# The down projection of a conditioned decoder layer as seven block products

## The chip, the cores and the metric

The kernel runs on one core of one Trainium2 chip, as one launch. The metric is device time in microseconds (us) of that core. All arithmetic is float32 at the interfaces; the engines are TensorE (PE, its weight loads PEld), VectorE (DVE), ScalarE (ACT), GpSimd (POOL) and SyncE (SP), which here only issues DMAs.

## The reference

The program is one inference step of a decoder layer with a DeltaNet branch, a sliding-window attention branch and a gated feed-forward part, for 1024 prompt tokens and 8 sample tokens (1032 columns in the kernel). Only the feed-forward part and the final norm bear on the change:

```python
h2 = _rmsnorm(x, lp['norm2_w']) * (1 + sc2) + sh2
gate = h2 @ lp['w_ffn_gate']                      # 1024 -> 2816
up = h2 @ lp['w_ffn_up']                          # 1024 -> 2816
gate_ext = jnp.concatenate([ffn_prev, gate], axis=1)
gc = _causal_dwconv(gate_ext, lp['ffn_conv_w'], L) + lp['ffn_conv_b']
x = x + gt2 * ((jax.nn.silu(gc) * up) @ lp['w_ffn_down'])   # 2816 -> 1024
...
y_prompt = _rmsnorm(xp, final_norm_w)
y_sample = _rmsnorm(xs, final_norm_w)
```

## The kernel before

**A product in float32.** Every operand of a large product is split in two parts: ScalarE copies it, rounded, as the high part (line 127), and VectorE subtracts that from the operand, which gives the low part (line 128). `mm3` then issues three matmuls for a tile: high by high (line 178), weight high by data low (179), weight low by data high (180). Data stand with features on the partitions and tokens along the columns. The 1032 columns are taken in four quarters of 256, 256, 260 and 260 (`QUARTERS`), the last eight of the last quarter being the sample tokens. A quarter of one row block of 128 outputs fills one bank of PSUM.

**Gate and up.** The 2816 features are 22 tiles of 128, taken as 11 pairs. For a pair, `pair_weights` loads two raw tiles of the weights and lets GpSimd make four of the weight sums (line 1525, buffers `ws`, three of them), which are split; `pair_product` then computes two feature tiles by two row halves by Strassen's seven products instead of eight, once for the first two quarters and once for the last two. Its operands stand split in rooms of 128 x 2080 elements, which fourteen tags name (`bmh0` to `bmh3`, `bml0` to `bml2`, `pk0` to `pk6`). ScalarE copies products that go to more than one place (line 1562), VectorE adds and multiplies at the end (lines 1605 to 1639). The result of the silu times up, `fa`, goes from SBUF to a DRAM tensor `act`, a half at a time, issued by SP.

**Down.** `ffn_down` takes the 22 feature tiles in groups of 4, 4, 4, 4, 2 and 4. For each tile it loads 128 rows of the weight (4 KB each) and the tile of `act`, both issued by SP, and splits both into rooms that the gate and up projections no longer need. Then, for each of 8 row blocks and 4 quarters, one bank collects the group's matmuls (twelve, or six for the group of two), in seven banks in turn, and VectorE adds the bank, times the gate, to the residual `x1` of that row block and quarter (`add_gated`, line 1406; for the sample columns lines 1410 and 1411, which go by a small tile `gtmp`). That is 192 such adds. Two of the row blocks of `x1` stay in SBUF from before; six are loaded from DRAM at the start of this stage, by ScalarE's queue. In the last group the quarters come in the order third, fourth, first, second, and after a quarter's last row block `norm_rows` does the final norm of its tokens: transposes on TensorE (line 188), sums of squares on ScalarE (line 1741), a scaling on VectorE and ScalarE (lines 1764 and 1761), and the output DMAs.

**The order.** A scheduler places the operations of the whole program on each engine's queue by due times, not by the order in the source, and can thus start the down projection's matmuls between the last ones of the up projection, or put a split ahead of an add. Each engine then runs its queue in that order; an instruction that waits holds up what stands behind it on the same engine.

## Time and profile before

| | us |
|---|---|
| three runs | 2182.31, 2189.14, 2196.92 |
| median | 2189.14 |
| the profiled execution | 2191.09 |
| its span | 2189.4 |

The windows of the profile cut the span by stage: up to 1485 us the two branches (the first row has the last part of them), from there to 1925 gate and up, to 2180 down and the final norm. Around the last two, whose own rows stand with the prediction:

```profile
1000.00:1485.00 485.00, 474.32 (x3435) 459.87 (x3434) 237.00 (x523) 146.52 (x330) 51.16 (x59) 0.96 0.45 132
2180.00:2189.40 9.40, 1.04 (x6) 0.42 (x4) 2.39 (x6) 3.07 (x10) 0.70 (x1) 0.81 0.30 112
```

A row gives the window, its length, busy us (and instructions) of PE, PEld, DVE, ACT and POOL, the clock that the throttle granted to TensorE as a share of full speed, the mean share of time in which the 16 DMA engines were busy, and the GB/s moved. In rows of instructions, "x2" behind a form is a count, the bracket is the engine's idle time ahead of it and what ended that, and buffer numbers are left out of the names.

### The profile page before, as it was taken

How to read it: one execution, taken by the hardware profiler on the slowest of the kernel's cores; microseconds unless marked ns; L12 is line 12 of the kernel's file. 1: busy time of each engine (PE TensorE's matmuls, PEld its weight loads, DVE VectorE, ACT ScalarE, POOL GpSimd, SP SyncE). 2: the span in 40 equal slices, each digit the busy share in tenths (PEclk: the TensorE clock that was granted, in tenths of full speed). 3: DMA queues.
4: the chain of work that ended last, by engine and by line, in shares of the span. 5: the costliest groups of instructions: out<-in, count | busy, mean ns of one | idle time of the engine just before them, and what ended most of it. 6: DMA issues, size and time to landing. Idle time of an engine off the chain costs nothing. (4 is left out here: it accounts for less than half of the span.)

```text
span 2189.4 us, 41264 instructions
## 1 busy us (share of the span) xinstructions
PE 2114.4 (97%) x16573; PEld 1996.0 (91%) x16573; DVE 1332.6 (61%) x2892; ACT 800.5 (37%) x2037; POOL 298.5 (14%) x395
## 2 busy tenths in 40 slices
PE   7999999999999999999999999999999999999998
PEld 4985887899898998898999999999999999999998
DVE  4656666374465655675324565478876876866565
ACT  3655446234234243333322032244433433421102
POOL 1000000021221111111110300002333232100000
PEclk8999999999999989999999999899999999999999
DMA  7256442141332222222226854413232222363202
GB/s 275 80 139 219 131 138 84 60 123 43 80 82 63 63 55 57 47 67 54 82 95 196 244 162 138 140 59 98 78 91 74 78 90 67 99 223 123 88 3 79
DMA packets 271346, 228.16 MB, mean 104 GB/s; under 512 B 57566, under 2 KB 237697, under 8 KB 271138
## 3 DMA queue, kind: packets, MB, share of 16 engines
q1 hardware_dynamic: 269826, 221.23, 33.4%
q10 hardware_dynamic: 1152, 3.70, 0.4%
q8 instruction: 130, 2.13, 0.4%
q14 instruction: 62, 0.51, 0.1%
q0 software_dynamic: 176, 0.59, 0.1%
HBM read 175.51 MB, written 52.35 MB: 104 GB/s over the span
## 5 line engine op out<-in xcount | busy, mean ns | idle before, releaser
L178 PE MATMUL mm<-b1h,wh 128*128 128x384 f32 (+1 forms) x1392 | 456.9, 329 | 4.6 <-ACT z L764 2.2
L180 PE MATMUL mm<-b1h,wl 128*128 128x384 f32 (+1 forms) x1392 | 452.2, 325 | 3.8 <-DVE wl L128 3.8
L179 PE MATMUL mm<-b1l,wh 128*128 128x384 f32 (+1 forms) x1392 | 449.8, 323 | 0.0
L178 PEld LDWEIGHTS mm<-b1h,wh 128*128 128x128 f32 x1392 | 263.1, 189 | 14.0 <-issue 4.7
L180 PEld LDWEIGHTS mm<-b1h,wl 128*128 128x128 f32 x1392 | 263.1, 189 | 10.3 <-issue 5.5
L179 PEld LDWEIGHTS mm<-b1l,wh 128*128 128x128 f32 x1392 | 263.5, 189 | 3.1 <-issue 2.8
L127 ACT ACTIVATE wh<-raw 128x1024 fp32r<-128x1024 f32 x75 | 78.6, 1048 | 157.9 <-PE mm L179 79.6
L128 DVE TENSOR_TENSOR wl<-raw,wh 128x1024 fp32r<-128x1024 f32 x74 | 90.4, 1221 | 66.0 <-ACT wh L127 65.3
L178 PE MATMUL mm<-pk,w 128*128 128x260 f32 (+1 forms) x440 | 124.4, 283 | 0.7 <-ACT pk L127 0.6
L179 PE MATMUL mm<-pk,w 128*128 128x260 f32 (+1 forms) x440 | 124.2, 282 | 0.8 <-DVE pk L128 0.8
L178 PE MATMUL mm<-b2h,wh 128*128 128x384 f32 (+1 forms) x384 | 123.3, 322 | 1.1 <-ACT wh L127 1.1
L180 PE MATMUL mm<-pk,w 128*128 128x260 f32 (+1 forms) x440 | 124.2, 282 | 0.0
L180 PE MATMUL mm<-b2h,wl 128*128 128x384 f32 (+1 forms) x384 | 121.9, 320 | 1.1 <-DVE wl L128 1.1
L179 PE MATMUL mm<-b2l,wh 128*128 128x384 f32 (+1 forms) x384 | 122.7, 320 | 0.0
L1406 DVE SCALAR_TENSOR_TENSOR x<-mm,mT,x 128x256 f32<-128x256 f32 (+2 forms) x133 | 63.4, 481 | 76.7 <-PE mm L180 74.5
L180 PE MATMUL mm<-bmh,pk 128*128 128x256 f32 (+1 forms) x380 | 109.8, 289 | 0.0
L178 PE MATMUL mm<-bmh,pk 128*128 128x260 f32 (+1 forms) x380 | 109.7, 289 | 0.0
L179 PE MATMUL mm<-bml,pk 128*128 128x260 f32 (+1 forms) x353 | 102.1, 289 | 0.0
L178 PE MATMUL mm<-bmh,w 128*128 128x260 f32 (+1 forms) x320 | 91.9, 287 | 0.0
L180 PE MATMUL mm<-bmh,w 128*128 128x260 f32 (+1 forms) x320 | 91.7, 287 | 0.0
L128 DVE TENSOR_TENSOR w<-ws,w 128x512 fp32r<-128x512 f32 x88 | 60.1, 684 | 41.6 <-ACT w L127 41.6
L178 PEld LDWEIGHTS mm<-pk,w 128*128 128x128 f32 x440 | 82.6, 188 | 1.4 <-ACT pk L127 0.8
(600 smaller groups left out, 5807.1 us busy)
## 6 DMA issues: line engine op xcount, KB each, us to landing
raw<-in_w_in_dram SPq DMA_DIRECT2D x60, 512.0 KB
bml<-act SPq DMA_DIRECT2D x22, 516.0 KB
raw<-in_w_ffn_gate_dram SPq DMA_DIRECT2D x22, 512.0 KB
raw<-in_w_ffn_up_dram SPq DMA_DIRECT2D x22, 512.0 KB
raw<-in_w_ffn_down_dram SPq DMA_DIRECT2D x22, 512.0 KB
qst<-in_w_mod_dram SPq DMA_DIRECT2D x16, 512.0 KB
raw<-in_w_mod_dram SPq DMA_DIRECT2D x16, 512.0 KB
raw<-in_x_prompt_dram SPq DMA_DIRECT2D x12, 512.0 KB
```

Source lines behind the costliest of these rows:

```text
L127: self.nc.scalar.activation(hi, x, AF.Copy)
L128: (eng or self.nc.vector).tensor_tensor(lo, x, hi.bitcast(F32), op=ALU.subtract)
L178: mm(ps, whi, xhi, start=first, stop=False, **kw)
L179: mm(ps, whi, xlo, start=False, stop=False, **kw)
L180: self.last_mm = mm(ps, wlo, xhi, start=False, stop=last, **kw).ins
L1406: nc.vector.scalar_tensor_tensor(x[:, :np_], ps[:, :np_], self.mT[:, m + j, 8:9], x[:, :np_], op0=ALU.mult, op1=ALU.add)
```

## The change

**What is computed.** The 22 feature tiles are again taken as 11 pairs, and the product of the weight (two feature tiles of a pair by two halves of 512 outputs) with the activations (two feature tiles by two halves of the columns) by Strassen's seven block products. One product of one pair is a step: four row blocks `j` times two column pieces `p`, so eight banks, three matmuls in each. A product keeps its eight banks, all that PSUM has, over all 11 pairs. Products 4 and 7 share their banks without a restart: after 4 the banks, which then hold product 4, are added to one quarter of the output, and after 7, holding the sum of both, to another; so it is with 3 and 5. The products are run in the order 4, 7, 3, 5, 1, 2, 6, which makes 77 steps. What stands in the banks after products 4, 7 and 6 goes to one quarter of the output, after 3, 5, 1 and 2 to two (`home`). For these ScalarE copies a bank to SBUF and VectorE adds the copy twice; for the former VectorE adds from the bank. `less` is the gate with its sign turned, for homes that subtract.

**Operands.** Five products need a sum or difference of two weight blocks; GpSimd makes it, in place, in the raw slot, from two blocks loaded by SP. Five of the seven activation operands are sums or differences too: GpSimd makes them during gate and up, as soon as a half of a pair is done (`act_operands`), into a tile `sums`, and issues a DMA of them to a new DRAM tensor `xd`, which takes the place of `act`; the other two go there by SP. Each step loads its operand, 128 x 516, and its weight block, 128 x 512, into one raw slot, which is split into one of 13 rooms. There are three raw slots and two halves of the tile `bmh0`. Before, a tile of `w` or `act` was loaded once; now a tile pair is read once for each product.

**The rest.** The six row blocks of `x1` are loaded by GpSimd's queue, behind the fetch of step 5, instead of ScalarE's. The last product runs bank after bank, 33 matmuls in each, in three banks in turn, the second piece of columns first, with the final norm woven in between. `copies`, a tile of the gate and up projections, is now also what ScalarE copies the banks to.

```diff
-    def add_gated(self, t, ps, j, m):
-
-        nc = self.nc
+    def add_gated(self, t, ps, j, m, by=None):
+
+        nc = self.nc
+        by = self.mT[:, m:m + 8, :] if by is None else by
         lo, n = QUARTERS[t]
         np_ = min(n, NP - lo)
         x = self.x1_cols(j, lo, n)
-        nc.vector.scalar_tensor_tensor(x[:, :np_], ps[:, :np_], self.mT[:, m + j, 8:9], x[:, :np_],
+        nc.vector.scalar_tensor_tensor(x[:, :np_], ps[:, :np_], by[:, j, 8:9], x[:, :np_],
                                        op0=ALU.mult, op1=ALU.add)
...
             done[p, i] += 1
-            if done[p, i] == 4:
-                c, n = HALF[p]
-                nc.sync.dma_start(self.act[f + i][:, c:c + n], a[i][:, c:c + n])
+            if done[p, 0] == done[p, 1] == 4:
+                self.act_operands(p, f // 2, a)
 
         self.pair_product(psum, w, (0, 1), up)
+
+    def act_operands(self, p, g, a):
+
+        nc = self.nc
+        c, n = HALF[p][0], QUARTERS[2 * p][1]
+        (a1, b1), (a2, b2) = ((x[:, c:c + n], x[:, c + n:c + 2 * n]) for x in a)
+        sums = self.sums[:, 5 * p:5 * p + 5, :n]
+        for i, x, y, op in ((0, a1, b2, ALU.add), (1, b1, b2, ALU.add), (2, a1, a2, ALU.add),
+                            (3, b1, a1, ALU.subtract), (4, a2, b2, ALU.subtract)):
+            nc.gpsimd.tensor_tensor(sums[:, i], x, y, op=op)
+        for i, x in ((5, a1), (6, b2)):
+            nc.sync.dma_start(self.xd[i, g][:, c // 2:c // 2 + n], x)
+        nc.gpsimd.dma_start(self.xd[0:5, g, :, c // 2:c // 2 + n].rearrange("i p n -> p i n"), sums)
...
-        for f0, f1 in ((0, 4), (4, 8), (8, 12), (12, 16), (16, 18), (18, FT)):
-            fs = range(f0, f1)
-            ws, acts = [], []
-            for f in fs:
-                raw = self.t(self.pw, [P, NP], "raw", bufs=3)
-                nc.sync.dma_start(raw, I["w_ffn_down"][0][f * P:(f + 1) * P, :])
-                ws.append(room(0, f, NP))
-                self.split(*ws[-1], raw)
...
-                if f == 0:
-                    for j in range(2, 8):
-                        nc.scalar.dma_start(self.x1[j], self.x1d[j])
...
-            order = [(j, t) for t in (2, 3, 0, 1) for j in range(8)] if last else \
-                [(j, t) for j in range(8) for t in range(4)]
-            for j, t in order:
...
-                for i, ((wh, wl), (ah, al)) in enumerate(zip(ws, acts)):
-                    self.mm3(ps, wh[:, j * P:(j + 1) * P], wl[:, j * P:(j + 1) * P], ah[:, c:c + n], al[:, c:c + n],
-                             i == 0, i == len(acts) - 1)
-                self.add_gated(t, ps, j, 40)
...
+        G, n = FT // 2, NT // 2
+        tags = ("bmh2", "bml0", "bml2", "bmh1", "pk2", "bml1", "pk3", "pk6", "pk4", "pk0", "pk5", "pk1", "bmh3")
+        made = {5: (2, (1, 1)), 3: (5, (0, 1), (1, 1), ALU.subtract), 4: (6, (1, 0), (0, 0), ALU.subtract),
+                7: (4, (1, 0), (1, 1), ALU.add), 1: (0, (0, 0), (1, 1), ALU.add), 2: (1, (0, 0)),
+                6: (3, (0, 0), (0, 1), ALU.add)}
+        chains = ((4, 7), (3, 5), (1,), (2,), (6,))
+        home = {3: ((0, 0, 1), (1, 1, 1)), 5: ((1, 0, 1), (0, 0, -1)), 4: ((0, 1, 1),), 7: ((0, 0, 1),),
+                1: ((0, 0, 1), (1, 1, 1)), 2: ((0, 1, 1), (1, 1, -1)), 6: ((1, 1, 1),)}
+        steps = [(i, g) for c in chains for i in c for g in range(G)]
+        ready = {}
+        less = []
+
+        def fetch(s):
+            i, g = steps[s]
+            if s % 5 == 3:
+                ready["raw"] = self.t(self.bm, [P, KC, QW], "bmh0").rearrange("p k n -> p (k n)")
+            raw = self.t(self.pw, [P, n + 512], "raw", bufs=3) if s % 5 < 3 else \
+                ready["raw"][:, (s % 5 - 3) * 1040:(s % 5 - 3) * 1040 + n + 512]
+            at, *src = made[i]
+            src = [x if type(x) is not tuple else
+                   I["w_ffn_down"][0][(2 * g + x[0]) * P:(2 * g + x[0] + 1) * P, 512 * x[1]:512 * x[1] + 512] for x in src]
+            nc.sync.dma_start(raw[:, n:], src[0])
+            if len(src) > 1:
+                other = self.t(self.pw, [P, 512], "ws", bufs=3)
+                nc.sync.dma_start(other, src[1])
+                nc.gpsimd.tensor_tensor(raw[:, n:], raw[:, n:], other, op=src[2])
+            nc.sync.dma_start(raw[:, :n], self.xd[at, g])
+            room = self.room(tags[s % len(tags)], [P, KC * QW])
+            hi, lo = room[:, :n + 512], room[:, n + 512:2 * (n + 512)]
+            self.split(hi, lo, raw)
+            ready[s] = hi, lo
+            if s == 5:
+                less.append(self.t(pool, [P, KC, 9], "less"))
+                nc.gpsimd.tensor_scalar(less[0], self.mT[:, 40:48, :], -1.0, None, op0=ALU.mult)
+                for j in (2, 3, 4):
+                    self.x1[j] = self.t(pool, [P, NT], f"x1_{j}")
+                for j in range(2, 8):
+                    nc.gpsimd.dma_start(self.x1[j], self.x1d[j])
+
+        def step(s, ps, p, j, first, last, kw):
+            hi, lo = ready[s]
+            x, w = slice(256 * p, 256 * p + 256 + 4 * p), slice(n + j * P, n + j * P + P)
+            self.mm3(ps, hi[:, w], lo[:, w], hi[:, x], lo[:, x], first, last, **kw)
+
+        def take(ps, i, p, j):
+            if len(home[i]) > 1:
+                self.turn = (self.turn + 1) % KC
+                r = self.copies[:, self.turn, :256 + 4 * p]
+                nc.scalar.copy(r, ps)
+                ps = r
+            for d, q, sign in home[i]:
+                self.add_gated(2 * p + q, ps, j + 4 * d, 40, self.mT[:, 40:48, :] if sign > 0 else less[0])
+
+        banks = [(self.pmm, "mm", 2), (psum, "wv", 2), (psum, "wy", 2)] * 2 + [(self.pmf, "mm", 1), (psum, "nr", 1)]
+        order = [(p, j) for j in range(4) for p in range(2)]
+        s = done = 0
+        for c in chains[:-1]:
+            ps = {(p, j): self.t(pl, [P, 512], tag, bufs=k)[:, :256 + 4 * p] for (p, j), (pl, tag, k) in zip(order, banks)}
+            for i in c:
+                for g in range(G):
+                    while done < min(s + len(tags), len(steps)):
+                        fetch(done)
+                        done += 1
+                    for p, j in order:
+                        step(s, ps[p, j], p, j, g == 0 and i == c[0], g == G - 1, {"skip_group_check": True} if i != c[0] else {})
+                        if g == G - 1:
+                            take(ps[p, j], i, p, j)
+                    s += 1
+        while done < len(steps):
+            fetch(done)
+            done += 1
+        self.ffn_rows(pool, psum)
+        tail = self.norm_rows(pool, psum, [2 * P, 3 * P])
+        chunks = [[0], [P], [], [], [4 * P, 5 * P], [6 * P, 7 * P, NP], [], []]
+        for k, (p, j) in enumerate((p, j) for p in (1, 0) for j in range(4)):
+            ps = self.t(self.pmf if k % 3 == 2 else self.pmm, [P, 512], "mm", bufs=1 if k % 3 == 2 else 2)[:, :256 + 4 * p]
+            for g in range(G):
+                step(s + g, ps, p, j, g == 0, g == G - 1, {})
+            take(ps, 6, p, j)
+            for c in chunks[k]:
+                for _ in self.norm_rows(pool, psum, [c]):
+                    pass
+            for _ in range({5: 6, 6: 1}.get(k, 0)):
+                next(tail)
+        for _ in tail:
+            pass
...
-            self.act = self.t(self.dr, [FT, P, NT], "act")
+            self.xd = self.t(self.dr, [7, FT // 2, P, NT // 2], "xd")
...
+                        self.sums = self.t(pool2, [P, 10, QW], "r")
...
-                                self.copies = self.t(pool2, [P, KC, QW], "r")
...
-            x1 = {j: self.t(pool, [P, NT], f"x1_{j}") for j in (5, 6, 7, 2, 3, 4)}
-            self.x1 = xj + [x1[j] for j in range(2, 8)]
+            x1 = {j: self.t(pool, [P, NT], f"x1_{j}") for j in (5, 6, 7)}
+            self.x1 = xj + [x1.get(j) for j in range(2, 8)]
```

Where the change moves instructions, in the order of each engine's queue. First GpSimd, one steady pair of the gate and up projections, before; `raw` are the two loaded weight tiles, `ws` the sums:

```order
L1525 TENSOR_TENSOR ws_18951<-raw_18931,ws_18941 128x512
L1525 TENSOR_TENSOR ws_19190<-raw_19180,raw_19182 128x512
L1525 TENSOR_TENSOR ws_19192<-ws_19190,raw_19180 128x512
L1525 TENSOR_TENSOR ws_19200<-raw_19180 128x512
L1525 TENSOR_TENSOR ws_19202<-raw_19182,ws_19192 128x512
L1525 TENSOR_TENSOR ws_19421<-raw_19411,raw_19413 128x512
```

and after, with `fa` the two feature tiles of the pair, `r` the tile `sums`, and `xd` the DRAM tensor:

```order
L1526 TENSOR_TENSOR ws_20758<-ws_20756,raw_20746 128x512
L1655 TENSOR_TENSOR r_15585<-fa_20038,fa_20039 128x256
L1655 TENSOR_TENSOR r_15585<-fa_20039 128x256
L1655 TENSOR_TENSOR r_15585<-fa_20038,fa_20039 128x260
L1655 TENSOR_TENSOR r_15585<-fa_20039 128x260
L1655 TENSOR_TENSOR r_15585<-fa_20038,fa_20039 128x256
L1655 TENSOR_TENSOR r_15585<-fa_20038 128x256
L1655 TENSOR_TENSOR r_15585<-fa_20038,fa_20039 128x260
L1655 TENSOR_TENSOR r_15585<-fa_20038 128x260
L1526 TENSOR_TENSOR ws_20766<-raw_20746 128x512
L1658 DMA xd_14275<-r_15585 128x5x256
L1658 DMA xd_14275<-r_15585 128x5x260
```

Between the second and the third weight sum of a pair there now stand eight operand sums (the other two are ahead of this piece), and the two DMAs stand behind the third. Next VectorE, where the down projection's first adds stand; `x_0` and `x_1` are row blocks of the residual, `pk` and `bml` rooms of split operands. Before:

```order
L128 TENSOR_TENSOR pk_2846_21386<-raw_21384,pk_2846_21386 128x1024
L1406 SCALAR_TENSOR_TENSOR x_0_2332_15579<-mm_20912,mT,x_0_2332_15579 128x256
L1406 SCALAR_TENSOR_TENSOR x_0_2332_15579<-wv_20926,mT,x_0_2332_15579 128x256
L128 TENSOR_TENSOR pk_2850_21396<-raw_21394,pk_2850_21396 128x1024
L1406 SCALAR_TENSOR_TENSOR x_0_2332_15579<-wy_20940,mT,x_0_2332_15579 128x260
L1406 SCALAR_TENSOR_TENSOR x_0_2332_15579<-mm_20954,mT,x_0_2332_15579 128x252
L1410 TENSOR_TENSOR gtmp_20968<-mm_20954,mT 128x8
L1406 SCALAR_TENSOR_TENSOR x_1_2333_15580<-mm_20971,mT,x_1_2333_15580 128x256
L128 TENSOR_TENSOR pk_2853_21405<-raw_21403,pk_2853_21405 128x1024
L1406 SCALAR_TENSOR_TENSOR x_1_2333_15580<-wv_20985,mT,x_1_2333_15580 128x256
L1406 SCALAR_TENSOR_TENSOR x_1_2333_15580<-wy_20999,mT,x_1_2333_15580 128x260
```

After, at the end of product 4:

```order
L128 TENSOR_TENSOR bml_2844_21226<-raw_21220,bml_2844_21226 128x1028
L128 TENSOR_TENSOR bmh_2847_21259<-raw_21253,bmh_2847_21259 128x1028
L128 TENSOR_TENSOR pk_2850_21292<-raw_21286,pk_2850_21292 128x1028
L1407 SCALAR_TENSOR_TENSOR x_0_2332_15579<-mm_20997,mT,x_0_2332_15579 128x256
L1407 SCALAR_TENSOR_TENSOR x_0_2332_15579<-wv_20998,mT,x_0_2332_15579 128x252
L1411 TENSOR_TENSOR gtmp_21467<-wv_20998,mT 128x8
L1407 SCALAR_TENSOR_TENSOR x_1_2333_15580<-wy_20999,mT,x_1_2333_15580 128x256
L1407 SCALAR_TENSOR_TENSOR x_1_2333_15580<-mm_21000,mT,x_1_2333_15580 128x252
L1412 TENSOR_TENSOR x_0_2332_15579<-x_0_2332_15579,gtmp_21467 128x8
L1411 TENSOR_TENSOR gtmp_21478<-mm_21000,mT 128x8
L1412 TENSOR_TENSOR x_1_2333_15580<-x_1_2333_15580,gtmp_21478 128x8
L128 TENSOR_TENSOR bml_2853_21325<-bmh_2851_21319,bml_2853_21325 128x1028
```

The adds, which came in at every bank of twelve matmuls between splits, now come eight in a row at the end of a product, behind the splits of steps up to the 18th. Last TensorE, in the down projection. Before, six of the twelve matmuls that one bank takes in a row over the four feature tiles of a group:

```order
L180 MATMUL wy_21148<-bmh_2794_20875,pk_2792_20870 128x256
L178 MATMUL wy_21148<-bml_2797_20890,pk_2796_20886 128x256
L179 MATMUL wy_21148<-bml_2797_20890,pk_2796_20886 128x256
L180 MATMUL wy_21148<-bml_2797_20890,pk_2796_20886 128x256
L178 MATMUL wy_21148<-bmh_2801_20900,pk_2799_20895 128x256
L179 MATMUL wy_21148<-bmh_2801_20900,pk_2799_20895 128x256
```

After, at the start of product 7, with rooms that hold steps 11 to 13:

```order
L178 MATMUL mm_20997<-bmh_2836_21128 128x256
L179 MATMUL mm_20997<-bmh_2836_21128 128x256
L180 MATMUL mm_20997<-bmh_2836_21128 128x256
L178 MATMUL mm_20997<-bmh_2839_21161 128x256
L179 MATMUL mm_20997<-bmh_2839_21161 128x256
L178 MATMUL wv_20998<-pk_2833_21119 128x260
```

Where a bank took its whole group of tiles, it now takes the three matmuls of one step or, as here, of two and part of a third, before the next bank gets its turn.

34 lines of the change are left out of this document (1 added, 33 removed).

## The prediction

> **What bounds the kernel now.** First the page's busy times and the chain of waits, then the stage that is changed by windows, then single instructions there. The page gives
>
> ```profile
> span 2189.4 us, 41264 instructions
> PE 2114.4 (97%) x16573; PEld 1996.0 (91%) x16573; DVE 1332.6 (61%) x2892; ACT 800.5 (37%) x2037; POOL 298.5 (14%) x395
> ```
>
> and the windows of the gate and up projections (first row) and of the down projection with the final norm (second row):
>
> ```profile
> 1485.00:1925.00 440.00, 436.49 (x3645) 435.17 (x3644) 339.37 (x582) 183.59 (x359) 124.15 (x122) 1.00 0.29 90
> 1925.00:2180.00 255.00, 255.00 (x2149) 254.33 (x2147) 149.36 (x356) 42.50 (x64) 3.86 (x7) 1.00 0.26 94
> ```
>
> The columns are length, then busy time and count of TensorE, its weight loads, VectorE, ScalarE and GpSimd, then granted clock, DMA share and GB/s. TensorE has no gap in the down projection, at a full clock, with VectorE at 149 of 255 us. So this stage lasts as long as its matmuls take, and a matmul less is time less. What one takes is read from the starts of three groups of twelve:
>
> ```profile
> 1903.98 0.28 PE L178 MATMUL mm<-bmh,w 128*128 128x256 f32 x1
> ...
> 1905.40 0.28 PE L178 MATMUL mm<-pk,w 128*128 128x260 f32 x1
> ...
> 1906.86 0.28 PE L178 MATMUL wv<-bml,w 128*128 128x256 f32 x1
> ```
>
> Twelve of 256 columns take 1.42 us and twelve of 260 take 1.46, so one takes 0.120 us. (The 0.28 us is latency; the next one starts inside it.)
>
> **What goes.** Before, the stage has 22 feature tiles x 8 row blocks x 4 quarters x 3 = 2112 matmuls. Afterwards it has 7 products x 11 tile pairs x 8 banks x 3 = 1848, with the same column counts. That is 264 fewer: 264 x 0.120 = **31.7 us**. One step (a product, a tile pair) is 24 matmuls, 2.88 us; 77 steps are 222 us.
>
> Banks now alternate every three matmuls, where they mostly held for twelve. At the seam of the two stages the trace already alternates:
>
> ```profile
> 1919.50 0.28 PE L179 MATMUL mm<-bml,pk 128*128 128x256 f32 x1
> 1919.62 0.28 PE L180 MATMUL wy<-bmh,pk 128*128 128x260 f32 x1
> ...
> 1919.98 0.28 PE L180 MATMUL mm<-bmh,pk 128*128 128x260 f32 x1
> ...
> 1920.34 0.28 PE L180 MATMUL wy<-bmh,pk 128*128 128x260 f32 x1
> ```
>
> A change every 0.36 us, three matmuls, leaves the spacing at 0.12. I cost it at nothing.
>
> **What is added per step, and what hides it.** Rows that carry the prices, by groups (count, then busy us and mean ns):
>
> ```profile
> L128 DVE TENSOR_TENSOR pk<-raw,pk 128x1024 fp32r<-128x1024 f32 x20 | 24.2, 1215 | 0.3 <-ACT pk L127 0.3
> L127 ACT ACTIVATE pk<-raw 128x1024 fp32r<-128x1024 f32 x20 | 21.0, 1056 | 129.1 <-PE mm L180 90.8 <-PE wv L180 33.6 <-DMA raw<-in_w_ffn_down_dram 4.8
> L1406 DVE SCALAR_TENSOR_TENSOR x<-mm,mT,x 128x256 f32<-128x256 f32 x48 | 22.9, 480 | 23.0 <-PE mm L180 22.9
> L1562 ACT COPY r<-mm 128x256 f32<-128x256 f32 x60 | 22.3, 372 | 39.2 <-PE mm L180 26.8 <-DVE w L128 12.5
> L1525 POOL TENSOR_TENSOR ws<-raw,raw 128x512 f32<-128x512 f32 x20 | 26.7, 1335 | 28.0 <-DVE ws L1525 21.0 <-DMA raw<-in_w_ffn_gate_dram 4.4 <-DVE w L128 1.2
> L1410 DVE TENSOR_TENSOR gtmp<-mm,mT 128x8 f32<-128x8 f32 x26 | 4.0, 154 | 0.0
> L1411 DVE TENSOR_TENSOR x<-x,gtmp 128x8 f32<-128x8 f32 x48 | 7.8, 163 | 1.0
> ```
>
> VectorE: 77 splits x 1.215 = 94 us; adds into the residual, 11 homes x 8 banks = 88 x 0.48 = 42; the sample columns 24 x (0.154 + 0.163) = 8. With some 12 for the final norm that is 156 us of 223, against 149 of 255 (44 splits, 192 adds). ScalarE: 77 x 1.056 = 81, plus 32 bank copies x 0.372 = 12. GpSimd: 55 of the 77 steps take the sum of two weight blocks, 55 x 1.335 = 73. All are under 2.88 us a step, and thirteen rooms let them run ahead.
>
> DMA: a step reads 264 KB of operands and one or two weight blocks of 262 KB, at most 788 KB in 2.88 us = 274 GB/s; the stage reads 55 MB where it read 23. What the engines can move, with 4 KB rows and (last row, mostly the modulation weights) 2 KB rows:
>
> ```profile
> 1925.00:1945.00 20.00, 20.00 (x171) 20.00 (x170) 13.64 (x31) 4.15 (x4) 0.00 (x0) 1.00 1.02 399
> 10.00:15.00 5.00, 4.12 (x22) 1.30 (x16) 0.84 (x2) 1.47 (x3) 0.19 (x1) 1.00 1.04 409
> ```
>
> So a step takes under 2 us of them. SyncE issues 209 DMAs x 0.33 (median below) = 69 us. How long a landing takes:
>
> ```profile
> L1675 SPq DMA_DIRECT2D bml<-act x22: 319/327/495, 1526.2 to 2070.1; - x22
> 1905.86 0.80 SPq L1675 DMA_DIRECT2D bml<-act  x2
> 1909.36 1.07 ACT L127 ACTIVATE bmh<-bml 128x1032 fp32r<-128x1032 f32 x1 [0.45 <-DMA bml<-act]
> ```
>
> Some 3.5 us from the first issue. One raw slot is held for three issues 1.0 + landing 3.5 + sum 1.34 + split 1.06 + 1.22 = 8.1 us. There are five slots, two of them halves of one tile that comes free as a whole, so I count four: one step per 2.0 us, under 2.88. The supply keeps up.
>
> **In the gate and up stage** GpSimd gets 110 operand sums of 256 or 260 columns. No row has that shape; the nearest, of 256 columns on 32 partitions, takes
>
> ```profile
> 547.93 0.74 POOL L996 TENSOR_TENSOR U<-G,upper 32x256 f32<-32x256 f32 x1 [1.94 <-DVE G L894]
> ```
>
> so between half of 1.335 and 0.74; with 0.74 they are 81 us on top of 124 in 440. In the issue order eight of the ten sums of a pair stand ahead of the third weight sum, 6 us that it waits; in the trace it runs 10 us before the next one can:
>
> ```profile
> 1600.77 1.29 POOL L1525 TENSOR_TENSOR ws<-raw 128x512 f32<-128x512 f32 x1 [3.79 <-DVE w L128]
> 1610.82 1.29 POOL L1525 TENSOR_TENSOR ws<-raw,ws 128x512 f32<-128x512 f32 x1 [8.76 <-DVE w L128]
> ```
>
> The fourth had to wait for a free buffer, 8.76 us. So the sums are covered there. The same sums hold VectorE up where it reads two SBUF operands:
>
> ```profile
> 1632.89 2.15 DVE L1639 TENSOR_TENSOR fa<-fa,r 128x256 f32<-128x256 f32 x2
> 1633.40 1.36 POOL L1525 TENSOR_TENSOR ws<-raw,raw 128x512 f32<-128x512 f32 x1
> 1634.96 0.68 DVE L128 TENSOR_TENSOR w<-ws,w 128x512 fp32r<-128x512 f32 x1
> ```
>
> Two such multiplies, some 0.4 us each alone, take 2.15 and end with the GpSimd sum. The Trainium skill, "SBUF — State Buffer", section "Who interferes with whom", says that a VectorE instruction with two SBUF inputs and a GpSimd instruction that reads SBUF exclude each other for a whole instruction; this row agrees. The new sums fall where a pair ends and the next begins, on VectorE's idle half. I take 1 us for all pairs, between 0 and 4.
>
> **What is given back.** At the ends of products 4 and 7 VectorE reads the eight banks itself: 8 x 0.48 + 4 x 0.32 = 5.1 us, and one or two splits in its queue (1.22 each) come between. TensorE comes back to the last bank 2.9 + 2.5 = 5.4 us after the first is done, so it waits 1 to 2 us; twice, 3 us. The issue order lets it run ahead on banks already read. After products 3, 5, 1 and 2 ScalarE copies a bank in 0.37 with at most one split of 1.06 between, inside 2.9: 1 us for all four. At the start (operands of the last pair, and six residual rows of 516 KB, issued by GpSimd behind its sums) I take 2; VectorE, queued behind those rows, would hold TensorE only after eleven steps, and by 4 us at most. The end is the same as now, one pair of chunks behind the last add: 0. Together with the 1 us above 7 us. Net 31.7 - 7 = 24.7 us. The profiled execution took 2191.1 us (2189.4 of span), 2.0 above the median of 2189.1, so I forecast 2164, and 2153 (little given back) to 2174 (twice as much and more).
>
> **Rivals.** (1) *VectorE becomes the bound.* If every weight sum shuts VectorE out for its full length, 55 x 1.335 = 73 us come on top of 156: 229 against 223 of TensorE, and then all takes stand behind late splits, some 10 us more: 16 beyond what I count, so 2180 (2172 to 2190). For it: the row above. Against: among adds and multiplies of that stage the pairs from SBUF average
>
> ```profile
> L1639 DVE TENSOR_TENSOR fa<-fa,r 128x260 f32<-128x260 f32 x30 | 22.0, 737 | 0.3
> L1639 DVE TENSOR_TENSOR fa<-fa,mm 128x260 f32<-128x260 f32 x11 | 4.6, 422 | 3.8 <-PE mm L180 3.8
> ```
>
> 0.3 us more than those with one operand in PSUM, not 1.3.
>
> (2) *Slower: the supply of operands sets the pace.* A slot's chain runs through DMA, GpSimd, ScalarE and VectorE in turn, each in program order. It decides once four slots need more than 4 x 2.88 = 11.5 us. With the 8.1 above, 2.6 of mutual shutting-out and a landing that doubles to 7 under three queued DMAs a step it is 14.2, or 3.6 a step; if queues behind one another add 2 more, 4.1. At 4.1 the 55 steps with a sum take 226 us and the other 22 63, together 289 instead of 222: 67 - 25 = 42 us slower, 2231; at 3.6 it is 55 x 0.72 = 40 less 25, 15 us slower, 2204. For it: three of the four links are new or doubled. Against: where the engines were full, a landing took
>
> ```profile
> 1924.29 0.49 SPq L1675 DMA_DIRECT2D bml<-act  x1
> 1927.55 1.07 ACT L127 ACTIVATE bmh<-bml 128x1032 fp32r<-128x1032 f32 x1 [0.97 <-DMA bml<-act]
> ```
>
> 3.3 us, and products 5 and 2 need no sum and let the rooms refill.
>
> (3) *The sums slow the gate and up stage.* With 2 us of TensorE waiting in each of 11 pairs: +22, 2186. Against: the order of TensorE, and all its products, are the same there, and ScalarE, which nothing shuts out, frees its banks.
>
> That the matmuls are not fewer can be left aside; the issue order has 264 less.
>
> **Numbers.** Forecast 0.62, rival 1 0.12, rival 2 0.22, rival 3 0.04. Within 1% of 2189 (what three runs spread over 2182 to 2197 can tell) means above 2167: of the forecast's 0.62 I put 0.47 below it and 0.15 above. Faster 0.47, the same 0.15 + 0.12 + 0.04 = 0.31, slower 0.22. The range 2150 to 2206 takes in all but most of rival 2.
>
> **What would show it.** Right: the down stage some 25 us shorter, TensorE's rows still 0.12 apart, waits of 1 to 3 us at the ends of products 4 and 7 released by VectorE's adds, none elsewhere; VectorE near 70% there; the gate and up stage unchanged within 4 us. Wrong: TensorE idle before each step, released by a split (rival 2, then behind it a DMA or a GpSimd sum); VectorE without a gap and its splits well over 1.3 us on average (rival 1); idle TensorE before 1925 us (rival 3). A granted clock under 1.00 after longer gaps would make any of them dearer.

## The result and the profile after

| | us |
|---|---|
| median of 14 runs, before in the same job | 2188.58 |
| median of 14 runs, changed kernel (2169.61 to 2184.77) | 2177.89 |
| ratio, 95% interval | 0.9949, 0.9932 to 0.9966 |
| forecast | 2164, range 2150 to 2206 |

The change makes the kernel faster by 11 us, where 24.7 were forecast. The page of the changed kernel, busy time and instructions of each engine:

```profile
span 2176.3 us, 41336 instructions
PE 2084.8 (96%) x16309; PEld 1960.8 (90%) x16309; DVE 1394.8 (64%) x2773; ACT 845.2 (39%) x2102; POOL 517.6 (24%) x589
```

TensorE has 264 instructions fewer and is busy 29.6 us less, but its idle time has grown. To leave out what differs ahead of the stage, I measure from the first wait of gate and up, which is in every run, to the last transposes of the final norm. TensorE's instructions before:

```profile
1490.03 0.39 PE L178 MATMUL mm<-pk,w 128*128 128x260 f32 x1 [0.58 <-ACT pk L127]
...
2181.00 0.80 PE L188 MATMUL wy<-ident,x 128*128 128x128 f32 x2 [0.62 <-ACT ws L1741]
```

and after, with the waits of 0.2 us and more between them (left out are two that both kernels have right behind the first):

```profile
1487.92 0.39 PE L178 MATMUL mm<-pk,w 128*128 128x260 f32 x1 [0.56 <-ACT pk L127]
...
1517.03 0.39 PE L178 MATMUL wv<-bml,w 128*128 128x256 f32 x1 [1.81 <-DVE bml L1638]
1523.95 0.39 PE L178 MATMUL mm<-bmh,w 128*128 128x260 f32 x1 [0.73 <-DVE fa L1640]
1527.31 0.39 PE L178 MATMUL wv<-pk,w 128*128 128x260 f32 x1 [1.41 <-DVE bml L1638]
1918.03 0.52 PE L178 MATMUL mm<-pk,w 128*128 128x256 f32 x1 [2.40 <-ACT bml L1563]
1926.96 0.39 PE L178 MATMUL wv<-bmh,w 128*128 128x260 f32 x1 [0.59 <-DVE bml L1638]
1931.35 0.39 PE L178 MATMUL mm<-bmh 128*128 128x260 f32 x1 [0.67 <-DVE fa L1640]
1935.32 0.39 PE L178 MATMUL wv<-bmh 128*128 128x260 f32 x1 [1.46 <-DVE bml L1638]
1937.55 0.38 PE L178 MATMUL wv<-bmh 128*128 128x256 f32 x1 [0.30 <-DVE bml L1638]
1960.06 0.38 PE L178 MATMUL mm<-pk 128*128 128x256 f32 x1 [0.44 <-DVE x L1407]
1963.47 0.39 PE L178 MATMUL mm<-pk 128*128 128x260 f32 x1 [1.12 <-DVE gtmp L1411]
1974.59 0.38 PE L178 MATMUL mm<-pk 128*128 128x256 f32 x1 [2.32 <-DVE x L1407]
2062.20 0.38 PE L178 MATMUL mm<-bml 128*128 128x256 f32 x1 [2.00 <-ACT bml L1714]
2167.74 0.80 PE L188 MATMUL wy<-ident,x 128*128 128x128 f32 x2 [0.98 <-ACT ws L1787]
```

From 1490.03 to 2181.00 are 691.0 us, from 1487.92 to 2167.74 679.8: 11.15 us less, which is the whole gain of the runs. Of the 31.7 us of matmuls saved, 20.5 were given back. The waits lie in four places: the **first pair** of gate and up (4.0 us; before, one of 0.8), the **seam** where gate and up end and the down projection begins (5.4), the **end of product 4** (0.4 + 1.1 + 2.3 = 3.9) and the **end of product 5** (2.0). Between the first pair and the seam there is none, and at the ends of products 7, 3, 1 and 2 none.

That is 14.4 us more than before. Another 2.9 us are two stretches in which matmuls start 0.215 us apart instead of 0.120, the one behind the wait at the seam (15 starts, 1.4 us), the other behind the one at 1974.59 (16 starts, 1.5 us):

```profile
1975.99 0.28 PE L180 MATMUL nr<-bmh 128*128 128x260 f32 x1
1976.11 0.38 PE L178 MATMUL mm<-bmh 128*128 128x256 f32 x1
1976.28 0.41 PE L179 MATMUL mm<-bmh 128*128 128x256 f32 x1
1976.50 0.41 PE L180 MATMUL mm<-bmh 128*128 128x256 f32 x1
...
1979.67 0.28 PE L180 MATMUL nr<-bml 128*128 128x260 f32 x1
```

The last transposes wait 0.4 us longer than before. That leaves 2.8 us. Some 1.8 of them belong to the waits: a wait is counted from the end of the last matmul, 0.28 us after its start, where the next would have started 0.12 after it, so each of the eleven further waits costs 0.16 us more than its bracket says. The last 1.0 us I have not located.

**The seam.** VectorE and GpSimd there, from the timeline of the changed kernel:

```profile
1917.03 1.27 POOL L1691 TENSOR_TENSOR raw<-raw,ws 128x512 f32<-128x512 f32 x1 [0.41 <-DMA raw<-in_w_ffn_down_dram]
1917.09 2.30 DVE L128 TENSOR_TENSOR bmh<-bmh,bmh 128x1028 fp32r<-128x1028 f32 x1
...
1920.45 1.80 DVE L1618 SCALAR_TENSOR_TENSOR fa<-fz,fcw,fa 128x512 f32<-128x512 f32 x1
1922.18 1.22 DVE L128 TENSOR_TENSOR bml<-raw,bml 128x1028 fp32r<-128x1028 f32 x1
1923.32 0.41 DVE L1638 TENSOR_TENSOR bml<-wv,bml 128x256 f32<-128x256 f32 x1
```

Splits of steps that TensorE will reach only some 20 us later (line 128) stand in VectorE's queue between the steps of the last pair's gate and up projections (lines 1618 and 1638) for which TensorE waits. A split beside a GpSimd sum takes 2.30 us, one without 1.22; the convolution step takes 1.80 (0.74 in most of this stage). The windows (length, busy us and count of PE, PEld, DVE, ACT, POOL, clock, DMA share, GB/s) show VectorE without a gap here, and the DMA engines near full for the 60 us behind it:

```profile
1910.00:1940.00 30.00, 24.58 (x185) 23.55 (x184) 30.00 (x30) 10.25 (x13) 20.66 (x15) 0.94 0.82 253
1940.00:1970.00 30.00, 28.45 (x237) 28.03 (x236) 21.41 (x21) 9.47 (x9) 23.26 (x21) 1.00 0.97 340
1970.00:2000.00 30.00, 27.68 (x220) 27.47 (x219) 17.80 (x22) 11.72 (x11) 19.14 (x12) 0.94 0.88 311
2000.00:2167.00 167.00, 164.76 (x1390) 163.69 (x1388) 127.29 (x196) 68.21 (x109) 42.73 (x31) 1.00 0.59 199
```

**The end of product 4.** The wait at 1974.59 in the timeline, followed back:

```profile
1957.50 3.27 POOL L1703 DMA_DIRECT2D x<-x1d  x6
...
1970.43 1.28 POOL L1691 TENSOR_TENSOR raw<-raw,ws 128x512 f32<-128x512 f32 x1 [7.13 <-DMA ws<-in_w_ffn_down_dram]
...
1971.75 1.06 ACT L127 ACTIVATE pk<-raw 128x1028 fp32r<-128x1028 f32 x1 [7.35 <-POOL raw L1691]
...
1972.84 1.23 DVE L128 TENSOR_TENSOR pk<-raw,pk 128x1028 fp32r<-128x1028 f32 x1 [6.09 <-ACT pk L127]
...
1974.07 0.47 DVE L1407 SCALAR_TENSOR_TENSOR x<-mm,mT,x 128x256 f32<-128x256 f32 x1
```

VectorE stood still for 6.1 us in front of a split whose weight block was late, and the add that frees TensorE's bank stood behind that split. GpSimd's sum in the second row waited for two blocks, which SP had issued among the residual rows:

```profile
1958.50 0.39 SPq L1687 DMA_DIRECT2D raw<-in_w_ffn_down_dram  x1
1959.58 0.33 SPq L1690 DMA_DIRECT2D ws<-in_w_ffn_down_dram  x1
```

The second was complete 10.7 us after its issue. I take a load's landing from the trace's record of its sixteen completions, the last of them. The ten loads of weight blocks and operands issued between 1956 and 1968 us took 6.3 to 13.6 us, with a median of 10.6; from 1895 to 1950 the median was 3.9, and in stretches of 30 us behind 2000 it was 4.2 to 5.4.

**The end of product 5** is the same on ScalarE. The copy that frees the bank stands behind a split; in ScalarE's rows:

```profile
2060.83 1.06 ACT L127 ACTIVATE bmh<-raw 128x1028 fp32r<-128x1028 f32 x1 [0.22 <-DMA raw<-xd]
2061.80 0.35 ACT L1714 COPY bml<-mm 128x256 f32<-128x256 f32 x1
```

### The profile page after: what moved, and what is told of

It is laid out like the page before. It is cut to its first block, busy times and chain, and to the rows that moved or that the text cites. A ratio compares the mean times of both kernels' runs of the same rounds, so it can differ in the third digit from the quotient of the medians.

```text
span 2176.3 us, 41336 instructions
## 1 busy us (share of the span) xinstructions
PE 2084.8 (96%) x16309; PEld 1960.8 (90%) x16309; DVE 1394.8 (64%) x2773; ACT 845.2 (39%) x2102; POOL 517.6 (24%) x589
## 5 line engine op out<-in xcount | busy, mean ns | idle before, releaser
L128 DVE TENSOR_TENSOR w<-ws,w 128x512 fp32r<-128x512 f32 x88 | 74.6, 849 | 36.5 <-ACT w L127 36.5
L1563 ACT COPY bml<-mm 128x256 f32<-128x256 f32 (+1 forms) x132 | 49.1, 373 | 104.1 <-PE mm L180 97.6
L178 PEld LDWEIGHTS mm<-pk,w 128*128 128x128 f32 x440 | 83.3, 189 | 3.8 <-ACT bml L1563 3.0
L179 PEld LDWEIGHTS mm<-pk,w 128*128 128x128 f32 x440 | 83.4, 190 | 1.0 <-DVE pk L128 1.0
L180 PEld LDWEIGHTS mm<-pk,w 128*128 128x128 f32 x440 | 83.6, 190 | 0.0
L1618 DVE SCALAR_TENSOR_TENSOR fa<-fz,fcw,fa 128x512 f32<-128x512 f32 x88 | 75.0, 860 | 0.4
```

The lines of the kernel that those rows point to most:

```text
L128: (eng or self.nc.vector).tensor_tensor(lo, x, hi.bitcast(F32), op=ALU.subtract)
L178: mm(ps, whi, xhi, start=first, stop=False, **kw)
L179: mm(ps, whi, xlo, start=False, stop=False, **kw)
L180: self.last_mm = mm(ps, wlo, xhi, start=False, stop=last, **kw).ins
L1563: nc.scalar.copy(r[p, i], x[p])
L1618: nc.vector.scalar_tensor_tensor(ai[:, c:e], zi[:, j + c:j + e], col(j), ai[:, c:e], op0=ALU.mult, op1=ALU.add)
```

## The experiments

"Stage" is the time from the first wait of gate and up to the last transposes, "waits" are TensorE's waits of 0.2 us and more in it, all from one profile of each run. Ratios are to the kernel before in the same job.

| run | ratio, 95% interval | stage | first pair | seam | behind it |
|---|---|---|---|---|---|
| before | | 691.0 | 0.8 | 0.0 | 0.0 |
| changed kernel | 0.9949, 0.9932 to 0.9966 | 679.8 | 4.0 | 5.4 | 5.9 |
| e1_no_weight_sums | 0.9917, 0.9895 to 0.9939 | 674.3 | 2.9 | 0.7 | 7.7 |
| e2_no_operand_sums | 0.9942, 0.9920 to 0.9965 | 677.5 | 6.8 | 6.6 | 0.6 |
| e3_spread_rows | 0.9942, 0.9924 to 0.9960 | 677.0 | 2.9 | 5.0 | 3.9 |
| e4_product2_first | 0.9947, 0.9929 to 0.9965 | 680.9 | 2.9 | 0.0 | 13.3 |
| e5_seam_order | 0.9941, 0.9922 to 0.9959 | 679.2 | 4.0 | 1.4 | 9.8 |
| e6_takes_first | 0.9959, 0.9943 to 0.9974 | 679.5 | 2.9 | 5.1 | 5.1 |
| e7_all_three | 0.9949, 0.9931 to 0.9967 | 678.1 | 3.2 | 1.5 | 7.6 |
| e8_seam_and_takes | 0.9942, 0.9920 to 0.9965 | 677.3 | 2.9 | 1.7 | 6.5 |
| e9_more_slots | 1.0012, 0.9999 to 1.0025 | 692.0 | 2.9 | 4.8 | 20.3 |
| e10_slots_and_orders | 0.9969, 0.9958 to 0.9979 | 685.3 | 2.9 | 1.2 | 18.3 |
| e11_slots_and_seam | 1.0011, 0.9999 to 1.0024 | 691.3 | 3.9 | 1.2 | 22.7 |
| e12_late_slots | 0.9907, 0.9888 to 0.9926 | 676.2 | 2.9 | 5.1 | 3.1 |
| e13_late_slots_orders | 0.9912, 0.9893 to 0.9931 | 677.4 | 2.9 | 2.4 | 8.3 |
| e14_late_slots_orders_rows | 0.9911, 0.9892 to 0.9930 | 675.9 | 4.0 | 2.3 | 5.9 |

The waits of the first pair come as 2.9 or as 4.0 us whatever was changed behind it. In the profiles with 2.9 some sixteen matmuls behind the wait of 1.8 us start 0.215 us apart, and in those with 4.0 none do: what the slow matmuls take, the later waits of that pair lack. A difference of 1 us there says nothing.

**One suspect at a time.**

```diff
-                nc.gpsimd.tensor_tensor(raw[:, n:], raw[:, n:], other, op=src[2])
```

> Leaves out the 55 GpSimd sums of two weight blocks in the down projection (the first block alone is used); every load stays. Theory A (GpSimd's sums stretch VectorE's instructions with two SBUF operands, which is what makes TensorE wait where the up projection ends): the five waits of TensorE between 1915 and 1940 us, 5.4 us in the changed kernel, fall to 1.5 or less, VectorE's splits there take 1.2 us each instead of 1.5 to 2.3, and the kernel is 5 to 8 us under the changed one, some 2171. Theory B (there are simply too many splits and adds at that place for VectorE, and GpSimd has no part): the waits stay at 4 us or more and the time within 2 us of the changed kernel. Theory C (the six residual rows hold up the operands): the wait of 2.3 us at 1974 us stays here under both.

Measured: the seam falls to 0.7 us. VectorE's splits of one form, in the changed kernel,

```profile
L128 DVE TENSOR_TENSOR pk<-raw,pk 128x1028 fp32r<-128x1028 f32 x25 | 35.8, 1431 | 18.7 <-ACT pk L127 18.6
```

and here:

```profile
L128 DVE TENSOR_TENSOR pk<-raw,pk 128x1028 fp32r<-128x1028 f32 x25 | 31.1, 1244 | 19.6 <-ACT pk L127 19.6
```

Theory A holds for the seam. What was not expected is one wait of 7.7 us at the end of product 4, in TensorE's rows:

```profile
1960.07 0.58 PE L178 MATMUL mm<-pk 128*128 128x256 f32 x1 [7.70 <-DVE x L1407]
```

and the window that holds it:

```profile
1950.00:1960.00 10.00, 2.37 (x20) 2.16 (x19) 4.07 (x5) 3.79 (x4) 0.00 (x0) 0.72 1.04 400
```

None of the engines is busy half the time there but the DMA engines, at 400 GB/s: TensorE came earlier to the same takings, and the splits ahead of them still waited for their operands. The stage is 5.5 us shorter than the changed kernel's, as theory A forecast, and nothing of that was won behind the seam.

```diff
-            nc.gpsimd.tensor_tensor(sums[:, i], x, y, op=op)
```

> Leaves out the 110 GpSimd operand sums in the gate and up projections (a zeroed tile is sent instead); all DMAs stay. Theory A: the three waits in the first pair (4.0 us against 0.8 before) go back to about 0.8, and the waits at the seam lose the share of the last pair's ten sums, 1 to 2 of 5.4 us; together 4 to 5 us under the changed kernel. Theory B: the seam stays at 5.4 us, and only the first pair gains, 3 us. If the waits of the first pair come from the DMAs and not from the sums, nothing changes.

Measured: inconclusive for the first pair. Without the sums the scheduler put the instructions of gate and up in another order, with other waits in the first pairs (6.8 us in all). The seam did not gain: 6.6 us, so the operand sums alone are not what makes it wait.

```diff
-                for j in range(2, 8):
+                for j in (2, 3):
                     nc.gpsimd.dma_start(self.x1[j], self.x1d[j])
...
+                if s in (20, 23, 26, 29):
+                    with self.tc.issue_after(summed.ins):
+                        nc.gpsimd.dma_start(self.x1[s // 3 - 2], self.x1d[s // 3 - 2])
```

> Four of the six residual rows are loaded behind the weight sums of steps 20, 23, 26 and 29 instead of all six in a row behind step 5's fetch. Theory C: the wait of 2.3 us at 1974 us goes (a split that waits for an operand queued behind 3.2 MB of rows, with two takings of banks behind it on VectorE), and with it the 3.4 us at half speed that follow, worth 1.6: 3 to 4 us under the changed kernel, some 2174; the seam keeps its 5.4 us. Rival: the operands are late there for GpSimd's or the slots' sake; then the wait stays at 1.5 us or more, and the time is the same within 1 us.

Measured: the waits at the end of product 4 are the same 3.9 us, in the same three pieces, at a DMA share of 1.03; the wait at the end of product 5 is gone. The longest landing of an operand or weight block between 1930 and 1980 us fell from 13.6 to 8.6 us, so the burst of rows does lengthen the landings. But shorter landings did not take the waits of product 4 away: theory C falls as it was put.

```diff
-        chains = ((4, 7), (3, 5), (1,), (2,), (6,))
+        chains = ((2,), (4, 7), (3, 5), (1,), (6,))
```

> Product 2, whose weight operand is one block and needs no GpSimd sum, runs first: 2, 4, 7, 3, 5, 1, 6. The same work; 11 of the 13 fetches that stand ahead at the seam then ask nothing of GpSimd. Theory A: the seam's waits fall from 5.4 us to 1.5 or less, 4 to 6 us under the changed kernel; product 2's taking (ScalarE copies) may cost up to 2 us more than product 4's. Theory B: the seam keeps 4 us or more, since as many splits stand there. All residual rows are needed after 11 steps instead of two of them: if the rows are the brake (theory C) the wait at the end of the first product grows beyond 2.3 us.

Measured: the seam has no wait at all, as theory A says, but one of 11.0 us stands at 1962, in the rows of ScalarE and TensorE:

```profile
1961.18 1.06 ACT L127 ACTIVATE pk<-raw 128x1028 fp32r<-128x1028 f32 x1 [7.70 <-DMA raw<-xd]
...
1962.30 0.58 PE L178 MATMUL mm<-pk 128*128 128x256 f32 x1 [11.01 <-ACT pk L127]
```

Product 2 takes an operand that GpSimd adds and sends through DRAM, and the last pair's was not there; product 4 takes one that SP sends as it is. The other 2.3 us in the table's last column are one wait at 2128 us.

**The order of the queues.** First, a split that is not needed yet may not stand ahead of the up projection's last multiply:

```diff
+            with self.tc.issue_after(self.last_up.ins) if s >= 6 else nullcontext():
+                self.split(hi, lo, raw)
```

> All work kept; only the order: VectorE's splits of step 6 and on stand behind the last multiply of the up projection instead of between its multiplies, and GpSimd's weight sums of those steps behind the first of the last pair's operand sums that the order allows. Theory A2 (at the seam VectorE is handed splits that nobody needs yet, each stretched by a GpSimd sum, ahead of adds and multiplies that TensorE waits for): the seam's waits fall from 5.4 us to 2 or less, worth 3 to 5 us with the clock that comes back; some 675 us from the first wait of gate and up to the last transposes, against 679.8 in the changed kernel and 691.0 before. Rival: the splits come late now and TensorE waits for them a few us further on, 3 us or more in front of steps 6 to 10; then the time is the same within 1 us.

The run moves GpSimd's queue as well (not in the lines above): the weight sums of those steps stand behind the last pair's operand sums.

Measured: with all work kept the seam falls from 5.4 to 1.4 us, and the end of product 4 from 3.9 to 2.2. TensorE, now 6 us ahead there, loses them again at the end of product 5, where ScalarE's copies stand behind splits of later steps:

```profile
2059.79 0.58 PE L178 MATMUL mm<-bml 128*128 128x256 f32 x1 [7.67 <-ACT bml L1716]
```

Second, no split of a step more than four beyond a product's end may stand ahead of that product's taking:

```diff
-                    while done < min(s + len(tags), len(steps)):
+                    while done < min(s + len(tags), len(steps) if i == 2 else s - g + G + 4):
...
+            with self.tc.issue_after(taken[-1].ins) if taken else nullcontext():
+                self.split(hi, lo, raw)
```

> All work kept; only the order: no split of a step more than four beyond the end of a product stands ahead of that product's taking of the banks, on VectorE (products 4, 7) or ScalarE (3, 5, 1). Theory D (the taking stands in an in-order queue behind splits whose operands have not landed): the waits at the ends of products 4, 7 and 3, 1.6 + 2.3 + 2.0 us in the changed kernel, fall to 1 us each or less, together 3 to 5 us under it with the half-speed stretch gone; the seam keeps its 5.4 us. Rival: TensorE then waits for the operands themselves, since the splits were only as late as the DMAs; then waits of the same size appear one to five steps later, and nothing is won.

Measured: between the seam and 2110 us TensorE does not wait once, through the ends of products 4, 7, 3, 5 and 1. Theory D holds for them. But it has 5.1 us of waits at the end of product 2, where the limit is lifted and the copies stand behind splits, in product 6, and in the norm woven into it. As I read it, fetching less far ahead left too little for product 6, which needs the operands of all 11 steps within 4 us.

> The two orders together with four of the six residual rows spread out. If the three causes are separate and are all: waits of TensorE after the first pair of 3 us or less in all, 667 to 670 us from the first wait of gate and up to the last transposes (the changed kernel's 679.8 less 5 for the seam, 4 for the takings, 2 for the rows), which is the 264 matmuls less the first pair's 3 us. If the DMAs are the limit behind all of them: 674 or more.

> The order at the seam together with takings first at the ends of products 4, 7, 3 and 5, but with no limit on fetching ahead during products 1 and 2, where the limit made operands late for the last product. All work kept. If takings and multiplies that stand behind early splits are the whole of it: waits after the first pair of 3 us or less in all, some 668 to 671 us from the first wait of gate and up to the last transposes (changed kernel 679.8). If the supply of operands sets the pace (theory S), whatever the order: the waits come back elsewhere, 675 or more.

Measured for these two (the second without the limit in products 1 and 2): the seam is down to 1.5 and 1.7 us, but waits come back, in e7_all_three at the ends of products 4 and 7 and in the last product, in e8_seam_and_takes at the ends of products 1 (1.1 us) and 2 (4.7 us). 678 and 677 us lie in the outcome that was named for the supply. The two waits of e8_seam_and_takes do not prove it: they are at the ends of the two products whose limit was lifted, and there the copies again stand behind splits.

**The supply.** Two more raw slots and two more tiles for second weight blocks:

```diff
+            raw = self.t(self.pw, [P, n + 512], "raw", bufs=3) if k < 3 else \
+                self.t(pool, [P, n + 512], "raw2", bufs=2) if k > 4 else \
...
+                other = self.t(self.pw, [P, 512], "ws", bufs=3) if s % 5 < 3 else \
+                    self.t(self.pw, [P, 512], f"w{s % 5 - 3}", bufs=1)
```

> Only the slots: two more raw slots and two more tiles for second weight blocks, so that more fetches are under way. All work kept. Theory S (a slot's chain of issue, landing of 6 to 7 us, sum, two halves of a split takes 11 to 13 us for four slots, so the operands hardly run ahead, and the splits ahead of a taking are late): the waits at the ends of products 4 and 5, 3.9 + 2.0 us, fall to 2 us in all, the seam stays at 5 us or grows; 674 to 677 us. If the DMAs' rate is the limit (share of 1.0 for 20 us around 1960): no gain, within 1 us of 679.8, and landings only grow longer.

> The slots, both orders and the four residual rows spread out. All work kept. Theory S with the seam: 667 to 670 us, waits after the first pair of 3 us or less. If the orders alone are enough: the same as with the two orders alone within 1 us. If the DMAs' rate is the limit: 674 or more, with waits while the share is 1.0.

> The slots and the order at the seam, takings left as they were. All work kept. Theory S: with the seam's 4 us gone and the supply further ahead, 670 to 673 us, and the 7.7 us that the order at the seam alone met at the end of product 5 does not come back. If takings must be put first in any case: a wait of 2 us or more stays at the end of product 4 or 5, 675 or more.

All three met one wait of 18 us, here in the rows of GpSimd and TensorE in e10_slots_and_orders:

```profile
1939.19 0.41 POOL L1709 TENSOR_SCALAR less<-mT 128x72 f32<-128x72 f32 x1 [3.02 <-DMA xd<-r]
...
1947.24 0.58 PE L178 MATMUL mm<-bml 128*128 128x256 f32 x1 [18.26 <-ACT bml L127]
```

`less` and the new slots belong to a pool whose place the last pair's sums hold until their DMA has landed, and, as I read it, the fetches of the later steps stood behind on SP's queue. Behind that wait e10_slots_and_orders has none at all. So these three told nothing of the slots' worth, and the next three use the new slots from step 13 on.

> Only the slots, two more raw slots and two more tiles for second weight blocks, used from step 13 on. All work kept. Theory S (supply hardly ahead): the seam keeps its 5 us; the waits behind it, 5.9 us in the changed kernel, fall to 2 us or less; 674 to 676 us from the first wait of gate and up to the last transposes (changed kernel 679.8). If the order alone matters: the waits behind the seam stay at 4 us or more, 679 to 681.

> The slots from step 13 on and the two orders (splits behind the up projection's multiplies at the seam; takings first at the ends of products 4, 7, 3 and 5). All work kept. Theory S: the waits of 1.1 and 4.7 us at the ends of products 1 and 2, which the two orders alone met, go; 669 to 672 us, waits behind the first pair of 3 us or less. If the DMAs' rate is the limit: 675 or more.

> As the last, and four of the six residual rows loaded behind the weight sums of steps 20, 23, 26 and 29. All work kept. If the rows' burst still matters once there is slack: 1 to 2 us less than without it; else the same within 1 us.

Measured: the slots alone leave two waits behind the seam, 3.1 us in all, the last of them before 1995 us, and none at the end of product 5. In e12_late_slots:

```profile
1964.98 0.58 PE L178 MATMUL mm<-bmh 128*128 128x256 f32 x1 [2.30 <-ACT bmh L127]
...
1994.93 0.38 PE L178 MATMUL mm<-pk 128*128 128x256 f32 x1 [0.84 <-DVE x L1407]
```

The stage of 676.2 us is just above the 674 to 676 that theory S named, and the 3.1 us lie between its 2 and the rival's 4. The ratio of 0.9907 (0.9888 to 0.9926) is the lowest of the kernels that keep all work, and its interval lies under that of the changed kernel. In microseconds, however, the medians of the three runs with late slots (2170.7 to 2171.8) are no lower than those of e3, e4, e5 and e8 (2171.2 to 2172.4): the kernel before took 2189.8 us in their job and 2183.8 to 2185.8 in the others. That the late slots beat those four is not shown.

With the two orders on top, the ends of products 1 and 2 wait 0.3 us in e13_late_slots_orders, where e8_seam_and_takes, with the same orders, waited 5.8: this part of theory S came. The rest did not. Both runs win at the seam and lose it to late operands, and in e13 also late residual rows, near 1960: e14_late_slots_orders_rows waits 5.9 us there in one piece, with the DMA engines at a share of 1.04 for the 15 us before. Its stage is 1.5 us shorter than e13's, the size named for rows that still matter.

Are the DMA engines the limit near 1960? In e1, e4, e13 and e14 the seam's waits fell, and single waits of 4.9 to 11.0 us came there while the engines were full. But e8_seam_and_takes has only 0.7 us of waits between 1940 and 1970, with the engines as full,

```profile
1940.00:1970.00 30.00, 29.18 (x240) 28.38 (x239) 16.90 (x25) 8.29 (x8) 16.93 (x15) 1.00 1.02 392
```

and e5_seam_order 2.2. So the load alone does not set these waits, and their cause stays open.

## Why the forecast had the sign and not the size

Of the 31.7 us, 20.5 were given back where 7 were forecast. The terms, in the forecast's own words:

- **264 matmuls fewer, 0.120 us each: right.** The count is as said, and the spacing keeps to 0.12 us with banks that alternate every three matmuls, except for the half-speed stretches.
- **"At the start (operands of the last pair, and six residual rows ...) I take 2": this step failed, 6.8 us (5.4 + 1.4 at half speed).** The sum set VectorE's work of the whole stage (156 us) against TensorE's (223 us). At the seam it is another account: between 1910 and 1940 us ten splits come on top of the last pair's work, and VectorE is busy 30.00 us of 30. Both halves of the cause are shown: without GpSimd's weight sums the waits fall to 0.7 us, and with them, but in the order of e5_seam_order, to 1.4. That run moved VectorE's splits and GpSimd's sums together; which of the two moves did it is not separated.
- **"One or two splits in its queue (1.22 each) come between ... twice, 3 us": mis-sized, 5.4 us (3.9 + 1.5 at half speed), at product 4 alone.** The queue was read rightly: adds behind splits. But a split in an in-order queue costs the time until its operand is there, 6.1 us of VectorE's time in the row at 1972.84, not its own 1.22. The rows above show it, and in e6_takes_first, which puts the adds first (and fetches less far ahead), these waits are gone. At product 7 the operands were there, and there was no wait. After products 3, 5, 1 and 2 I took 1 us; it is 2.0, at product 5 alone.
- **"Some 3.5 us from the first issue ... 8.1 us ... The supply keeps up": up to 2000 us it only kept pace, behind that it did as forecast.** The landing was the mis-sized part: a median of 10.6 us for the loads issued beside the residual rows, and some 5 later. The sums took 1.65 instead of 1.34 and the splits 1.52 (mean over all 76 behind 1905 us) instead of 1.22. A slot's chain was thus 1.0 + 10.6 + 1.65 + 1.07 + 1.52 = 15.8 us beside the rows and, with a landing of 5, 10.2 later, for four slots, where four steps take 11.5. The run-ahead agrees. Counted from the trace (splits that have ended, less steps whose matmuls have started), operands stood five to seven steps ahead from 1930 to 2000 us without gaining, and eight to twelve from 2020 to 2110, of thirteen rooms. So the wait at the end of product 5 came with operands ten steps ahead: the copy stood behind a split that was not needed for long. It is a matter of the queue's order: e6_takes_first has no wait there. More slots removed it too (e12_late_slots).
- **Gate and up, 1 us: 3.1 more than before, all in the first pair.** The pairs between the first and the last have no wait, as forecast, although the operand sums took 1.04 us each, 114 us in all, where I had 0.74 and 81. That the operand sums cause it is not shown, since the run without them changed the order as well.
- **The last part of the stage at nothing: nearly right, 0.4 us.** The other 2.8 us, most of them the restarts behind the waits, were not in the sum.
- **The rivals.** Rival 1's price (a weight sum shuts VectorE out for its full length) was far too high over the stage: 76 x 0.3 = 23 us of longer splits, not 73, and VectorE is busy 0.76 of the time behind 2000 us. It was right as a local matter. The Trainium skill, "SBUF — State Buffer", section "Who interferes with whom", by which a VectorE instruction with two SBUF inputs and a GpSimd instruction that reads SBUF contend, is borne out by the splits: 1.43 against 1.24 us on average, 2.30 against 1.22 singly. Rival 2 (four slots need more than 11.5 us) held only beside the residual rows, for some 12 us of issues; with a run-ahead to draw on it cost a few us there, not 0.7 a step. Rival 3 did not come.

The four places were not independent. A cure brought TensorE to the next place earlier, where the splits were hardly earlier: e5_seam_order won 4 us at the seam and lost 5.7 at the end of product 5. The stages shortened most are those of e1 (5.5 us), e14 (3.9) and e12 (3.6), kernels without weight sums or with more slots. But e13, with the slots too, won 2.4, and e3, with neither, 2.8, and each is one profile: that an earlier supply is what pays is likely, not shown.

## What to carry to other kernels

Where a product is cut into fewer matmuls, the matmuls saved are certain and the price lies at the boundaries: read, for each place where a stage begins or a bank is emptied, what stands ahead of the freeing instruction in its engine's queue, and price it by when its operand lands, not by its duration. Set the slot's chain (issue, landing, every engine it passes) against the number of slots times the step, and take the landing under the load of that very stretch: here it was 3.9 us in one and 10.6 in the next. Count also how many steps the operands are ahead. Where they are far ahead and a bank is still freed late, it is the order of the queue that has to change, not the supply.

## What the runs showed of the hardware that was not expected

- After waits of TensorE of 2.3 and 2.4 us, matmuls of 256 and 260 columns started 0.215 us apart for 3.3 us, as in the rows at 1976.11 to 1979.67, which adds 1.4 to 1.5 us to the wait. After the wait of 2.0 us at 2062 they did not, nor after one of 2.35 us in e13_late_slots_orders, and after the one of 1.8 us in the first pair they did in ten of fourteen profiles. The Trainium skill, "TensorE: Matmul & The Clock Gate", section "Part 1: The HAM clock gate (the "warmup" mystery)", names about 3.4 us as an idle window that throttles the clock; the gaps here were shorter.
- A load of some 256 KB landed 6.3 to 13.6 us after its issue while the DMA engines ran at a share near 1.0 beside six residual rows, against the 3.3 us in the forecast's row, taken when the engines had just become full. With four of the six rows spread out (e3_spread_rows) the longest was 8.6 us, so at least a part of the difference is what was queued beside it.
